# Four weight sums of a fast convolution moved from VectorE to ScalarE and an accumulating DMA, with the set-up in another order

## The chip, the cores and the metric

The kernel runs on one core of a Trainium2 chip. The metric is device time in microseconds: the median of three runs before is 747.08 us (746.89 to 747.51). A core has five engines with a queue each: TensorE (PE in the profile; its weight loads are PEld), VectorE (DVE), ScalarE (ACT), GpSimd (POOL) and SyncE (SP). An engine takes its instructions in order; semaphores tie the queues together.

## The reference

A causal convolution in time with eight matrix taps: each output row is a sum of eight input rows, each times a 512x512 matrix.

```python
B, S, D, K = 8, 4096, 512, 8          # x: (B, S, D), kernel: (K, D, D)
for k in range(K):
    shifted = x if k == 0 else np.concatenate([np.zeros((B, k, D)), x[:, :-k, :]], axis=1)
    out += np.matmul(shifted, kernel[k])
```

## The kernel before

**Layout.** The 32,768 rows are cut into 128 runs of 256 rows (16 runs per batch). A run is one partition's work: a matmul handles one time position of all 128 runs at once. `XR` is a ring of 20 time positions in transposed form (input features on partitions); a slice of it, or of a sum of such slices, is the stationary operand, and a weight tile of 128x512 in bf16 is the moving one. A product of a 512-wide input and a weight is four matmuls (`product`, L115). The result lands in a half of a PSUM pair (`pair`, two halves of 128x512 f32); there are four pairs.

**Arithmetic.** The first 4 positions of a run are computed directly with all eight taps (`direct`, 32 products). The other 252 are 21 steps of 12 positions. A step combines two groups of four taps, H1 and H0, with three groups of four positions by four nodes: PL uses the sum of the weight groups, MI their difference, H1 and H0 themselves. Inside a node four taps meet four positions, again by sums: weights have indices (b, c), each LO, HI or MID, where a MID weight is a difference of two others. For PL, MI and H1 a node is nine products: u (weight MID, MID), a0 and a1 (MID, LO and MID, HI), v0 and v1 (LO, MID and HI, MID), and l00, l01, l10, l11. H0 is a leaf: u, a0, a1 and eight more, so W[H0, LO, MID] and W[H0, HI, MID] aren't needed. The inputs of these products are sums of rows that VectorE makes: z, then A and s from z, and F from s.

**Course of a node.** a1 opens a PSUM pair q; ScalarE copies its half 1 to half 0 (L171, for the leaf L168 with a sign); u is added to half 1 and a0 to half 0. ScalarE then copies half 1 into two further pairs p0 and p1 (the seeds: L187, and L189 with a sign) and half 0 into the SBUF tile DT (`node_dts`, L193). TensorE adds v0 and v1, VectorE makes the other halves from DT (`node_d`), TensorE adds the l products, and `node_e` takes the pairs out: for PL by ScalarE (L229), for the others by VectorE. Node k is `nodes[k]`, counted from 1: node 1 is PL, 2 MI, 3 H1, 4 H0 of the first step, 5 PL of the second.

**Weights.** Eight taps are loaded by GpSimd's DMA queue with a cast to bf16 (`load_w`). All other weight tiles are made on the chip, once: 9 tiles for PL and MI each and the MID tiles of H1 and H0, by VectorE (`wsum` is a difference, `plus` a sum, both of 128x2048 bf16).

**Set-up.** Input rows come in two ways. Rows 0 to 11 of each run and the last seven rows of the run before (the history, for the first positions) are loaded by GpSimd or SyncE into tiles that later hold weights (`xin`, `H`, `XF`), transposed by TensorE into PSUM (`transpose_pe`, names x0, x4, x8, x9, h4, h3) and copied into `XR` by ScalarE (`here`, L296; `history`, L292, and a memset by VectorE). Later rows go to DRAM as bf16 (`load_x`) and into `XR` by SyncE's transposing DMA (`transpose_x`). `fill` issues two matmuls on a zero tile whose result isn't used. The first steps aren't a loop: the order of all instructions, for each queue, is the order of the calls from `pd = ...` (L378) to `go(4, "d1")` (L595), written out. `go(k, name)` is one act of node k's slot, and in it acts of the nodes after it; go(2, "s0"), say, is seed 0 of node 3, and go(2, "u") its u. From node 5 on a loop over `SLOT` (L597) gives the order. A load on GpSimd's queue waits for the landing of the one eight before it.

Of the kernel before, what the change touches and what calls it, by code (L numbers as in the profile page):

```python
# [14 lines left out]
def kernel(  # L15
# [64 lines left out]
    def tt(o, a, b, op):  # L80
        nc.vector.tensor_tensor(out=o, in0=a, in1=b, op=op)  # L81
# [7 lines left out]
    def rows(o, t, n):  # L89
        load(o, xr[:, t:t + n, :])  # L90
# [56 lines left out]
    def node_A(n):  # L147
        tt(AX[n.k % 2], n.z[:, n.o + 2:n.o + 4], n.z[:, n.o + 3:n.o + 5], ADD)
# [24 lines left out]
    def node_a0(n):  # L173
        product(n.q[:, 0], comps(n)[1][0], W[n.a, MID, LO], False)
# [76 lines left out]
    def load_w(tap):  # L251
        n = K - 1 - tap
        load(W[n >> 2, n >> 1 & 1, n & 1], kr[:, :, tap, :])

    def wsum(a, b_, c_):
        o = W[a, b_, c_]
        if a == MI and b_ != MID and c_ != MID:
            tt(o, W[H0, b_, c_], W[H1, b_, c_], SUB)
        elif b_ == c_ == MID:
            tt(o, W[a, MID, LO], W[a, MID, HI], SUB)  # L260
        elif b_ == MID:
            tt(o, W[a, HI, c_], W[a, LO, c_], SUB)
        else:
            tt(o, W[a, b_, LO], W[a, b_, HI], SUB)
# [7 lines left out]
    def fill(pw):  # L272
        for h in range(2):
            nc.tensor.matmul(pw[:, h], lhsT=zero[:, 0:P], rhs=zero, start=True, stop=True)  # L274

    def transpose_pe(name, k, src, t0, t1):
        o = pair(k).bitcast(bf).rearrange("p a (b d) -> p (a b) d", b=2)
        for t in range(t0, t1):
            for c in range(DC):
                nc.tensor.transpose(o[:, t - t0, c * P:(c + 1) * P], src[:, t, c * P:(c + 1) * P],  # L280
                                    ident)
        bank[name] = o[:, 0:t1 - t0]
# [7 lines left out]
    def history(eng, t, name):  # L290
        z = XR[:, place(t):place(t) + bank[name].shape[1]]
        eng(out=to(z), in_=prev(bank[name]))  # L292
        nc.vector.memset(z[:, :, 0:D:G], 0.0)

    def here(eng, t, name, a, b):
        eng(out=XR[:, place(t) + a:place(t) + b], in_=bank[name][:, a:b])  # L296
# [18 lines left out]
    def seed_plus(b_, c_):
        nc.scalar.copy(out=W[PL, b_, c_], in_=W[H1, b_, c_])

    def seed_minus(b_, c_):
        nc.scalar.mul(out=W[MI, b_, c_], in_=W[H1, b_, c_], mul=-1.0)

    def add_h0(a, b_, c_):
        nc.gpsimd.dma_start(out=W[a, b_, c_], in_=W[H0, b_, c_], accum_op=ADD)
# [50 lines left out]
    def go(k, name):  # L373
        there, act = step(k)[name]
        if there:
            act()

    pd = {0: pair(0), 1: pair(1)}  # L378
    load_w(0)
    rows(H[:, 4:8], RUN - 4, 4)  # L380
    make_identity(nc, ident)
    nc.vector.memset(zero, 0.0)
    nc.sync.dma_start(out=XF, in_=xr[:, 0:4, :])
    cast(nc.vector.tensor_copy, 2, 4)
    for k in range(7):
        fill(pair(2 + k % 2))
    go(3, "v1")
    cast(nc.scalar.copy, 0, 2)
    transpose_pe("x0", 2, xin[0], 0, 4)
    load_w(4)  # L390
    here(nc.scalar.copy, 0, "x0", 2, 4)
    go(3, "d0")
    load_w(5)
    load_w(1)
    here(nc.scalar.copy, 0, "x0", 0, 2)
    fill(pair(3))
    load_w(7)
    fill(pair(3))
    direct(0, 3)
    direct(0, 2)  # L400
    fill(pair(2))
    transpose_pe("h4", 3, H, 4, 8)
    history(nc.scalar.copy, -4, "h4")
    load_w(3)
    plus((HI, HI))
    wsum(H1, HI, MID)
    wsum(MI, HI, HI)
    plus((HI, LO))
    wsum(MI, HI, LO)
    direct(0, 1)  # L410
    direct(0, 0)
    direct(4, 3)
    fill(pair(2))
    wsum(PL, HI, MID)
    direct(4, 0)
    direct(4, 2)
    direct(4, 1)
    wsum(H1, MID, LO)
    wsum(MI, HI, MID)
    plus((LO, LO))  # L420
    direct(5, 3)
    wsum(MI, LO, LO)
    wsum(PL, MID, LO)
    load_w(6)
    direct(1, 0)
    rows(H[:, 1:4], RUN - 7, 3)
    direct(1, 3)
    direct(5, 1)
    direct(5, 2)
    direct(1, 1)  # L430
    direct(7, 3)
    direct(1, 2)
    direct(3, 3)
    direct(3, 2)
    direct(3, 0)
    wsum(H0, MID, LO)
    load_w(2)
    load_xin(4)
    wsum(H1, LO, MID)
    wsum(H1, MID, HI)  # L440
    wsum(H1, MID, MID)
    direct(6, 2)
    direct(3, 1)
    transpose_pe("h3", 2, H, 1, 4)
    history(nc.scalar.copy, -7, "h3")
    direct(6, 3)
    load_xin(8, 0, 2)
    direct(2, 2)
    direct(7, 2)
    plus((LO, HI))  # L450
    direct(2, 0)
    transpose_pe("x4", 3, xin[4], 0, 4)
    direct(2, 1)
    direct(7, 0)
    load_xin(8, 2, 4)
    wsum(PL, MID, HI)
    transpose_pe("x8", 2, xin[8], 0, 2)
    here(nc.scalar.copy, 4, "x4", 0, 2)
    here(nc.scalar.copy, 4, "x4", 2, 4)
    fill(pair(3))  # L460
    transpose_pe("x9", 2, xin[8], 2, 4)
    direct(7, 1)
    direct(6, 1)
    wsum(MI, LO, HI)
    direct(5, 0)
    wsum(PL, LO, MID)
    direct(6, 0)
    load_x(12)
    here(nc.scalar.copy, 8, "x8", 0, 2)
    wsum(MI, MID, HI)  # L470
    wsum(PL, MID, MID)
    wsum(MI, LO, MID)
# [8 lines left out]
    node_a1(nodes[1])
    load_x(20)
    load_x(24)
    s_rows(nodes[1], 0, 3)
    direct(2, 3)
    node_u(nodes[1])
    node_seed(nodes[1], 0)
    node_seed(nodes[1], 1)
    node_a0(nodes[1])
    node_dts(nodes[1])  # L490
    s_rows(nodes[1], 3, 5)
    transpose_x(12)
    node_z(nodes[2])
    node_A(nodes[2])
# [6 lines left out]
    wsum(MI, MID, LO)
    wsum(MI, MID, MID)
    node_a1(nodes[2])
    direct_out(1)
    go(1, "l00")
    go(1, "s")
    go(1, "l01")
    go(1, "e0")
    go(1, "a0")
    go(1, "dt")  # L510
    go(1, "u")
    go(1, "s0")
    go(1, "z")
    go(1, "F0")
    go(1, "A")
# [10 lines left out]
    go(1, "e1")
    wsum(H0, MID, HI)
    go(1, "a1")
    go(1, "d1")
    go(2, "s")  # L530
    go(2, "l00")
    go(2, "l01")
    go(2, "a0")
    go(3, "v0")
    go(2, "dt")
    go(2, "e0")
    go(2, "z")
    go(2, "u")
    go(2, "s0")
    go(2, "l10")  # L540
    go(2, "s1")
    go(1, "x")
    go(2, "x")
    wsum(H0, MID, MID)
# [16 lines left out]
    go(3, "l10")
    go(3, "s")
    go(3, "z")
    go(3, "A")
    go(3, "l11")
    go(3, "e1")
    go(4, "l01")
    go(3, "s1")
    go(3, "d1")
    go(4, "l00")  # L570
    go(4, "s")
    go(3, "dt")
    go(4, "b1")
    go(4, "l10")
    go(3, "g0")
# [4 lines left out]
    go(4, "s0")  # L580
    go(4, "a0")
    go(4, "s1")
    go(4, "F0")
    go(4, "dt")
    go(4, "z")
    go(4, "A")
    go(4, "v0")
    go(4, "l11")
# [41 lines left out]
```

## Time and profile before

| | |
|---|---|
| median of three runs | 747.08 us |
| profiled execution, its own time | 746.51 us |
| its span, from the first to the last instruction | 744.8 us |
| TensorE busy | 729.3 us, 98% |
| VectorE busy | 697.2 us, 94% |
| ScalarE busy | 241.3 us, 32% |
| GpSimd busy | 57.8 us, 8% |
| share of the chain that ended last: PE | 93% |

Busy time counts the time in which an engine works at an instruction. Matmuls overlap one another, and their ends are modelled, so a hole of TensorE is read best from one start to the next. The chain that ended last is followed back from the last instruction, at each step to what released it or to the instruction before it on its engine. A row of a timeline gives the start, the length, the engine, the line, the operation, the tiles (written <- read) and the count, and in brackets the idle time before it and what ended it.

### The profile page before, as it was taken

How to read it: one execution, taken by the hardware profiler on the slowest of the kernel's cores; microseconds unless marked ns; L12 is line 12 of the kernel's file. 1: busy time of each engine (PE TensorE's matmuls, PEld its weight loads, DVE VectorE, ACT ScalarE, POOL GpSimd, SP SyncE). 2: the span in 40 equal slices, each digit the busy share in tenths (PEclk: the TensorE clock that was granted, in tenths of full speed). 3: DMA queues.
4: the chain of work that ended last, by engine and by line, in shares of the span. 5: the costliest groups of instructions: out<-in, count | busy, mean ns of one | idle time of the engine just before them, and what ended most of it. 6: DMA issues, size and time to landing. Idle time of an engine off the chain costs nothing.

```text
span 744.8 us, 8881 instructions
## 1 busy us (share of the span) xinstructions
PE 729.3 (98%) x3354; PEld 331.0 (44%) x3422; DVE 697.2 (94%) x729; ACT 241.3 (32%) x369; POOL 57.8 (8%) x98
## 2 busy tenths in 40 slices
PE   8989999999999999999999999999999999999997
PEld 3444444444444444444444444444444444444443
DVE  2999999999999999999999999999999999999996
ACT  3053233332333333232423333242333323333331
POOL 5200010101010010101011010101101010100000
PEclk9999999999999999999999999999999999999999
DMA  9996859696877969697795969688596968865414
GB/s 199 210 214 161 225 118 251 136 234 162 203 205 163 236 145 235 156 219 182 185 231 138 233 152 236 165 181 239 137 240 142 241 164 188 220 148 179 139 78 170
DMA packets 159372, 138.88 MB, mean 186 GB/s; under 512 B 130144, under 2 KB 134240, under 8 KB 159200
## 3 DMA queue, kind: packets, MB, share of 16 engines
q1 hardware_dynamic: 145456, 99.89, 49.6%
q0 software_dynamic: 13728, 38.15, 28.0%
q8 instruction: 27, 0.44, 0.2%
q10 hardware_dynamic: 144, 0.26, 0.1%
q14 instruction: 17, 0.14, 0.1%
HBM read 77.33 MB, written 99.09 MB: 237 GB/s over the span
## 4 chain that ended last, share of the span: by engine, by line
PE 93%; ACT 1%; issue 1%; DVE 1%; DVEq 0%; ACTq 0%
PE pp L117 92%; ACT pp L187 0%; DVE w L81 0%; PE pp L280 0%; ACT DT L193 0%; ACT XR L296 0%; DVE pp L81 0%; DVE pp L206 0%; DVE y L81 0%; ACT pp L189 0%; DVEq L625 0%; ACT pp L168 0%; ACT pp L171 0%; PE pp L274 0%; DVE F L81 0%
## 5 line engine op out<-in xcount | busy, mean ns | idle before, releaser
L117 PE MATMUL pp<-w,S 128*128 128x512 bf16 x1153 | 269.0, 379 | 1.5
L117 PE MATMUL pp<-w,F 128*128 128x512 bf16 x986 | 248.4, 379 | 1.0
L117 PEld LDWEIGHTS <-S 128*128 128x128 bf16 x1176 | 114.8, 98 | 140.2 <-issue 3.6
L117 PE MATMUL pp<-w,A 128*128 128x512 bf16 x659 | 170.5, 379 | 2.7 <-ACT pp L189 1.2
L81 DVE TENSOR_TENSOR Z<-XR 128x2048 bf16<-128x2048 bf16 (+3 forms) x109 | 154.6, 1437 | 0.1
L117 PEld LDWEIGHTS <-F 128*128 128x128 bf16 x1008 | 98.6, 98 | 119.0
L81 DVE TENSOR_TENSOR S<-Z 128x2560 bf16<-128x2560 bf16 (+1 forms) x85 | 124.8, 1469 | 0.0
L187 ACT COPY pp<-pp 128x512 f32<-128x512 f32 x84 | 57.3, 682 | 158.8 <-PE pp L117 154.0
L117 PEld LDWEIGHTS <-A 128*128 128x128 bf16 x672 | 65.2, 97 | 82.8 <-DVE A L81 4.5
L171 ACT COPY pp<-pp 128x512 f32<-128x512 f32 x63 | 35.9, 570 | 198.9 <-PE pp L117 198.9
L117 PE MATMUL pp<-w,Z 128*128 128x512 bf16 x330 | 85.4, 379 | 1.7 <-ACT DT L193 1.4
L81 DVE TENSOR_TENSOR F<-S 128x1024 bf16<-128x1024 bf16 x126 | 86.6, 687 | 0.0
L106 POOL COPY junk<-A 128x2 bf16<-128x2 bf16 x18 | 17.6, 980 | 557.4 <-DVE A L81 557.4
L232 DVE SCALAR_TENSOR_TENSOR y<-pp,y 128x1024 f32<-128x1024 f32 x42 | 51.3, 1222 | 8.9 <-PE pp L117 8.4
L81 DVE TENSOR_TENSOR A<-Z 128x1024 bf16<-128x1024 bf16 x84 | 57.9, 690 | 1.5
L189 ACT ACTIVATE pp<-pp 128x512 f32<-128x512 f32 x84 | 58.1, 692 | 1.1 <-PE pp L117 1.1
L206 DVE SCALAR_TENSOR_TENSOR pp<-pp,DT 128x512 f32<-128x512 f32 x63 | 43.9, 697 | 14.5 <-PE pp L117 14.5
L229 ACT ACTIVATE y<-pp 128x1024 f32<-128x1024 f32 x42 | 43.1, 1027 | 40.3 <-PE pp L117 40.1
L81 DVE TENSOR_TENSOR y<-y,pp 128x1024 f32<-128x1024 f32 (+1 forms) x43 | 51.1, 1190 | 2.0 <-PE pp L117 1.9
L81 DVE TENSOR_TENSOR y<-pp,y 128x1024 f32<-128x1024 f32 x42 | 51.2, 1219 | 1.7 <-DMA out_dram<-y 1.7
L117 PEld LDWEIGHTS <-Z 128*128 128x128 bf16 x336 | 32.9, 98 | 41.4 <-issue 1.5
L247 DVE SCALAR_TENSOR_TENSOR y<-y 128x1024 f32<-128x1024 f32 x42 | 51.2, 1219 | 0.0
(28 smaller groups left out, 244.9 us busy)
## 6 DMA issues: line engine op xcount, KB each, us to landing
out_dram<-y SPq DMA_DIRECT2D x127, 512.0 KB, 7.7
xd<-in_x_dram POOLq DMA_DIRECT2D x61, 512.0 KB, 10.8
w<-in_kernel_dram POOLq DMA_DIRECT2D x8, 512.0 KB, 15.9
w<-in_x_dram SPq DMA_DIRECT2D x1, 1024.0 KB, 4.9
w<-in_x_dram POOLq DMA_DIRECT2D x2, 512.0 KB, 14.9
XR<-xd SPq DMA_TRANSPOSE x61, 5.4
w<-in_x_dram POOLq DMA_DIRECT2D x2, 256.0 KB, 18.4
w<-in_x_dram POOLq DMA_DIRECT2D x1, 384.0 KB, 20.3
```

Source lines behind the costliest of these rows:

```text
L81: nc.vector.tensor_tensor(out=o, in0=a, in1=b, op=op)
L106: nc.gpsimd.tensor_copy(out=junk, in_=z[:, 0:2])
L117: nc.tensor.matmul(bank, lhsT=comp[:, c * P:(c + 1) * P], rhs=w[:, c, :], start=start and c == 0, stop=c == DC - 1, skip_group_check=True)
L171: nc.scalar.copy(out=n.q[:, 0], in_=n.q[:, 1])
L187: nc.scalar.copy(out=o, in_=q)
L189: nc.scalar.mul(out=o, in_=q, mul=-1.0)
L206: nc.vector.scalar_tensor_tensor(out=p[:, 0], in0=p[:, 1], scalar=-1.0, in1=DT, op0=MUL, op1=SUB)
L229: nc.scalar.mul(out=cc[b_], in_=p, mul=0.5)
L232: nc.vector.scalar_tensor_tensor(out=dd[b_], in0=p, scalar=-0.5, in1=cc[b_], op0=MUL, op1=ADD)
L247: nc.vector.scalar_tensor_tensor(out=cc[b_], in0=cc[b_], scalar=2.0, in1=dd[b_], op0=MUL, op1=SUB)
```

## The change

Four weight tiles, W[H0, MID, HI], W[H0, MID, LO], W[H0, MID, MID] and W[H1, LO, MID], which VectorE made as a difference p - m, are now made in two steps: ScalarE writes -m into the tile (`wminus`), and a DMA on GpSimd's queue adds p to it (`wplus`, `accum_op=ADD`). Which two tiles are p and m stands in `terms`. Three helpers that were not called are gone. The calls of the set-up stand in another order: the taps are loaded 0, 1, 4, 5, 2, 6, 3, 7 instead of 0, 4, 5, 1, 7, 3, 6, 2, rows 4 to 11 before the last four taps, the history rows first; the direct products follow the taps; the row sums of nodes 1 and 2 stand among the weight sums; and the first acts of nodes 1 to 4 are permuted. The fills are 13 in both.

```diff
+    def terms(a, b_, c_):
+        if a == MI and b_ != MID and c_ != MID:
+            return W[H0, b_, c_], W[H1, b_, c_]
+        if b_ == c_ == MID:
+            return W[a, MID, LO], W[a, MID, HI]
+        if b_ == MID:
+            return W[a, HI, c_], W[a, LO, c_]
+        return W[a, b_, LO], W[a, b_, HI]
+
     def wsum(a, b_, c_):
-        o = W[a, b_, c_]
...
+        p, m = terms(a, b_, c_)
+        tt(W[a, b_, c_], p, m, SUB)
+
+    def wminus(a, b_, c_):
+        nc.scalar.mul(out=W[a, b_, c_], in_=terms(a, b_, c_)[1], mul=-1.0)
+
+    def wplus(a, b_, c_):
+        nc.gpsimd.dma_start(out=W[a, b_, c_], in_=terms(a, b_, c_)[0], accum_op=ADD)
```

The new order of the set-up, up to node 3, with what was there before left out:

```python
    nc.vector.memset(zero, 0.0)
    make_identity(nc, ident)
    nc.sync.dma_start(out=XF, in_=xr[:, 0:4, :])
    for k in range(7):
        fill(pair(2 + k % 2))
    fill(pair(3))
    ...
    rows(H[:, 4:8], RUN - 4, 4)
    ...
    load_xin(4)
    transpose_pe("x4", 3, xin[4], 0, 4)
    here(nc.scalar.copy, 4, "x4", 0, 2)
    load_xin(8, 0, 2)
    transpose_pe("x8", 2, xin[8], 0, 2)
    direct(1, 3)
    load_xin(8, 2, 4)
    transpose_pe("x9", 2, xin[8], 2, 4)
    here(nc.scalar.copy, 4, "x4", 2, 4)
    ...
    here(nc.scalar.copy, 8, "x8", 0, 2)
    wsum(PL, HI, MID)
    z_rows(nodes[1], 0, 5)
    ...
    wminus(H0, MID, HI)
    load_w(6)
    ...
    node_z(nodes[2])
    direct(3, 1)
    wminus(H1, LO, MID)
    wsum(MI, LO, HI)
    direct(6, 0)
    node_A(nodes[2])
    wminus(H0, MID, LO)
    plus((LO, LO))
    wsum(PL, MID, LO)
    wplus(H0, MID, LO)
    node_a1(nodes[1])
    ...
    node_seed(nodes[1], 0)
    node_v(nodes[1], 0)
    wsum(MI, MID, HI)
    node_a1(nodes[2])
    node_v(nodes[1], 1)
    ...
    go(1, "a1")
    go(1, "d0")
    go(1, "F0")
    go(1, "v1")
    load_x(20)
    go(1, "e1")
    wminus(H0, MID, MID)
    go(2, "u")
    go(1, "d1")
    wplus(H0, MID, MID)
    go(2, "s0")
    go(2, "a0")
```

Before, the corresponding calls around node 3 stood so: `go(2, "a0")`, `go(3, "v0")`, `go(2, "dt")`, `go(2, "e0")`, `go(2, "z")`, `go(2, "u")`, `go(2, "s0")`; and `wsum(MI, MID, HI)` stood ahead of node 1's z.

More of the change, by code (lines that the diff above doesn't have):

```diff
@@ L253, in load_w @@
         load(W[n >> 2, n >> 1 & 1, n & 1], kr[:, :, tap, :])
-    def wsum(a, b_, c_):
-        o = W[a, b_, c_]
[L257 to L264, printed above, removed]
+    def terms(a, b_, c_):
[6 more added lines that the diff above has]
+        return W[a, b_, LO], W[a, b_, HI]
+    def wsum(a, b_, c_):
+        p, m = terms(a, b_, c_)
[4 more added lines that the diff above has]
+        nc.gpsimd.dma_start(out=W[a, b_, c_], in_=terms(a, b_, c_)[0], accum_op=ADD)
     def plus(*which):
@@ L313, in direct_out @@
         store(2 * b_, y)
[L315 to L322, printed above, removed]
     def z_rows(n, a, b):
@@ L378 @@
     pd = {0: pair(0), 1: pair(1)}
-    load_w(0)
-    rows(H[:, 4:8], RUN - 4, 4)
+    nc.vector.memset(zero, 0.0)
     make_identity(nc, ident)
-    nc.vector.memset(zero, 0.0)
     nc.sync.dma_start(out=XF, in_=xr[:, 0:4, :])
-    cast(nc.vector.tensor_copy, 2, 4)
+    go(3, "v0")
     for k in range(7):
         fill(pair(2 + k % 2))
-    go(3, "v1")
+    fill(pair(3))
+    cast(nc.vector.tensor_copy, 2, 4)
+    rows(H[:, 4:8], RUN - 4, 4)
     cast(nc.scalar.copy, 0, 2)
     transpose_pe("x0", 2, xin[0], 0, 4)
-    load_w(4)
@@ L391 @@
-    here(nc.scalar.copy, 0, "x0", 2, 4)
-    go(3, "d0")
-    load_w(5)
-    load_w(1)
-    here(nc.scalar.copy, 0, "x0", 0, 2)
-    fill(pair(3))
[L397 to L407, printed above, removed]
-    plus((HI, LO))
[L409 to L413, printed above, removed]
@@ L414 @@
-    wsum(PL, HI, MID)
[L415 to L472, printed above, removed]
+    here(nc.scalar.copy, 0, "x0", 0, 2)
+    load_w(0)
+    here(nc.scalar.copy, 0, "x0", 2, 4)
+    fill(pair(3))
+    transpose_pe("h4", 3, H, 4, 8)
+    fill(pair(2))
+    direct(0, 1)
+    rows(H[:, 1:4], RUN - 7, 3)
@@ new lines @@
+    fill(pair(2))
+    transpose_pe("h3", 2, H, 1, 4)
+    history(nc.scalar.copy, -4, "h4")
+    direct(0, 2)
+    history(nc.scalar.copy, -7, "h3")
+    load_w(1)
+    direct(0, 3)
+    direct(0, 0)
+    direct(1, 0)
+    go(3, "v1")
+    load_w(4)
+    load_w(5)
+    wsum(MI, HI, HI)
+    plus((HI, HI))
+    direct(1, 1)
+    direct(1, 2)
+    direct(4, 2)
+    wsum(H1, HI, MID)
+    direct(4, 0)
+    direct(4, 3)
+    wsum(MI, HI, LO)
+    direct(4, 1)
+    direct(5, 2)
+    direct(5, 0)
+    load_xin(4)
@@ L473 @@
+    transpose_pe("x4", 3, xin[4], 0, 4)
+    go(4, "x")
+    here(nc.scalar.copy, 4, "x4", 0, 2)
+    load_xin(8, 0, 2)
+    go(3, "d0")
+    transpose_pe("x8", 2, xin[8], 0, 2)
+    direct(1, 3)
+    load_xin(8, 2, 4)
+    transpose_pe("x9", 2, xin[8], 2, 4)
+    here(nc.scalar.copy, 4, "x4", 2, 4)
+    direct(5, 1)
+    fill(pair(3))
+    load_w(2)
+    plus((HI, LO))
+    wsum(MI, HI, MID)
+    direct(2, 2)
+    direct(2, 1)
+    here(nc.scalar.copy, 8, "x8", 0, 2)
+    wsum(PL, HI, MID)
     z_rows(nodes[1], 0, 5)
-    load_x(16)
@@ L475 @@
-    node_A(nodes[1])
+    direct(2, 3)
     here(nc.scalar.copy, 10, "x9", 0, 2)
     z_rows(nodes[1], 5, 7)
+    s_rows(nodes[1], 3, 5)
     fill(pair(2))
-    go(4, "F1")
-    direct_out(0)
[L481 to L486, printed above, removed]
-    node_seed(nodes[1], 0)
[L488 to L494, printed above, removed]
@@ L495 @@
-    node_F(nodes[1], 0)
+    wminus(H0, MID, HI)
+    load_w(6)
+    s_rows(nodes[1], 0, 3)
+    node_F(nodes[1], 0)
+    load_w(3)
+    node_A(nodes[1])
+    plus((LO, HI))
+    load_w(7)
+    direct(2, 0)
+    wplus(H0, MID, HI)
+    direct(6, 2)
+    wsum(PL, MID, HI)
+    direct(6, 3)
+    node_z(nodes[2])
+    direct(3, 1)
+    wminus(H1, LO, MID)
+    wsum(MI, LO, HI)
+    direct(6, 0)
+    node_A(nodes[2])
+    wminus(H0, MID, LO)
+    plus((LO, LO))
+    wsum(PL, MID, LO)
+    wplus(H0, MID, LO)
@@ L496 @@
+    node_a1(nodes[1])
+    direct(5, 3)
+    direct(7, 0)
+    wsum(PL, MID, MID)
+    direct(3, 0)
+    wplus(H1, LO, MID)
+    direct(3, 3)
+    direct(6, 1)
+    wsum(PL, LO, MID)
+    wsum(MI, LO, LO)
+    direct(7, 1)
+    wsum(H1, MID, HI)
+    node_u(nodes[1])
+    load_x(12)
+    go(3, "d1")
+    wsum(MI, MID, LO)
+    node_a0(nodes[1])
+    direct(3, 2)
+    direct_out(0)
+    node_seed(nodes[1], 1)
+    go(1, "s")
+    node_dts(nodes[1])
+    direct(7, 2)
+    node_seed(nodes[1], 0)
     node_v(nodes[1], 0)
+    wsum(MI, MID, HI)
@@ L497 @@
+    node_a1(nodes[2])
+    node_v(nodes[1], 1)
     node_d(nodes[1], 0)
+    wsum(MI, MID, MID)
     go(1, "F1")
-    node_v(nodes[1], 1)
-    node_d(nodes[1], 1)
[L501 to L508, printed above, removed]
+    go(1, "z")
+    direct(7, 3)
+    go(1, "A")
+    go(1, "l01")
+    go(1, "u")
+    go(1, "l00")
+    direct_out(1)
+    go(1, "s0")
+    node_d(nodes[1], 1)
     go(1, "a0")
@@ L510 @@
     go(1, "dt")
[L511 to L515, printed above, removed]
+    go(1, "e0")
     go(1, "l11")
+    transpose_x(12)
+    wsum(MI, LO, MID)
+    wsum(H1, MID, LO)
     go(1, "s1")
-    load_x(28)
+    wsum(H1, MID, MID)
+    load_x(16)
     go(1, "l10")
     go(1, "v0")
-    load_x(32)
+    go(1, "a1")
+    go(1, "d0")
+    go(1, "F0")
     go(1, "v1")
+    load_x(20)
+    go(1, "e1")
+    wminus(H0, MID, MID)
+    go(2, "u")
+    go(1, "d1")
+    wplus(H0, MID, MID)
@@ L523 @@
+    go(2, "s0")
+    go(2, "a0")
+    go(2, "s")
     go(3, "F0")
-    go(1, "d0")
+    go(2, "l00")
     go(2, "F1")
[L526 to L531, printed above, removed]
-    go(2, "l01")
[L533 to L544, printed above, removed]
+    go(2, "z")
+    go(2, "dt")
+    go(2, "l01")
@@ L547 @@
     go(2, "d0")
-    go(2, "v1")
-    go(2, "d1")
-    go(2, "a1")
+    go(2, "l10")
+    go(2, "e0")
+    go(1, "x")
+    go(3, "s")
     go(2, "l11")
+    go(2, "s1")
     go(2, "A")
     go(3, "l00")
+    go(3, "l01")
+    go(2, "a1")
+    go(2, "v1")
+    go(2, "e1")
     go(3, "F1")
-    go(3, "l01")
+    go(3, "a0")
+    go(2, "d1")
+    go(3, "e0")
     go(3, "u")
-    go(2, "e1")
-    go(3, "e0")
-    go(3, "a0")
-    go(3, "s0")
[L561 to L565, printed above, removed]
+    go(3, "s1")
+    go(3, "z")
+    go(4, "s")
+    go(3, "A")
+    go(3, "l10")
+    go(3, "dt")
+    go(3, "l11")
+    go(4, "z")
+    load_x(24)
+    load_x(28)
+    go(4, "F0")
+    go(2, "x")
+    go(3, "g0")
+    load_x(32)
+    go(3, "s0")
     go(3, "e1")
+    go(4, "l11")
+    go(4, "l10")
+    go(4, "l00")
+    go(4, "b1")
     go(4, "l01")
[L568 to L575, printed above, removed]
     go(4, "u")
-    go(4, "x")
+    go(4, "a0")
+    go(4, "s0")
     go(4, "e0")
-    load_x(36)
[L580 to L588, printed above, removed]
+    go(4, "g1")
+    go(4, "s1")
+    go(4, "v0")
+    go(4, "A")
+    go(4, "v1")
+    go(4, "dt")
+    go(4, "d0")
+    go(4, "F1")
+    load_x(36)
+    go(4, "d1")
     go(3, "r")
-    go(4, "g1")
-    go(4, "v1")
-    go(4, "d0")
+    go(4, "a1")
     go(4, "e1")
-    go(4, "a1")
-    go(4, "d1")
     for k in range(5, len(nodes)):
```

## The prediction

> **What bounds the kernel now.** I read TensorE's busy time by stage first, then its waits, then the engines' timelines over the first 90 us. By stage (range, length, busy with count, clock, DMA share, GB/s):
>
> ```profile
> 0.00:20.00 20.00, 17.64 (x89) 1.00 1.03 199
> 20.00:40.00 20.00, 18.44 (x110) 1.00 1.15 211
> 40.00:60.00 20.00, 17.89 (x86) 1.00 1.01 216
> 60.00:80.00 20.00, 19.22 (x88) 1.00 0.54 121
> 80.00:100.00 20.00, 19.18 (x88) 1.00 0.93 246
> ```
>
> TensorE is the bound from start to end: the chain that ended last is 93% PE, and from 200 to 700 us it is busy 99.5 of every 100 us. All loops after the set-up are untouched and the number of matmuls is equal (26 fills and 76 transposes among them), so the change is worth what it does to TensorE's holes before about 90 us. Four of the holes in TensorE's timeline:
>
> ```profile
> 40.07 0.61 PE L280 MATMUL pp<-ident,w 128*128 128x128 bf16 x8 [0.67 <-ACT XR L296]
> ...
> 48.38 1.02 PE L117 MATMUL pp<-w,A 128*128 128x512 bf16 x4 [1.21 <-ACT pp L189]
> ...
> 63.91 1.02 PE L117 MATMUL pp<-w,Z 128*128 128x512 bf16 x4 [0.68 <-ACT DT L193]
> ...
> 82.05 1.02 PE L117 MATMUL pp<-w,A 128*128 128x512 bf16 x4 [0.70 <-ACT pp L187]
> ```
>
> A row is a group, its start, length, and in brackets the idle time and what ended it. The idle time counts from a modelled end; start to start, less 0.216 per matmul, each hole is 0.16 longer. So counted, before loses 0.63 in four small holes up to 12.8 us, then 0.83 (15.31), 0.33 (32.29), 0.85 (34.00), 0.83 (40.07), 1.38 (48.38), 0.89 (55.31), 0.84 (63.91), 0.87 (82.05): 7.45 us.
>
> None of these waits for a weight sum. Most wait for ScalarE, and three show a rule needed below. At 63.91 the product u writes half 1 of node 3's PSUM pair, but waits for DT's copy, which reads half 0; at 48.38 and 82.05 a0 writes half 0 and waits for seeds that read half 1. A product waits for every reader of its pair queued before it, whichever half. ScalarE and VectorE:
>
> ```profile
> 36.83 1.93 ACT L296 COPY XR<-pp 128x1024 bf16<-128x1024 bf16 x2 [4.10 <-PE pp L280]
> 39.01 1.01 ACT L296 COPY XR<-pp 128x1024 bf16<-128x1024 bf16 x1 [0.25 <-PE pp L280]
> ...
> 60.74 0.57 ACT L171 COPY pp<-pp 128x512 f32<-128x512 f32 x1 [1.62 <-PE pp L117]
> 63.27 0.59 ACT L193 COPY DT<-pp 128x512 f32<-128x512 f32 x1 [1.97 <-PE pp L117]
> ```
>
> ```profile
> 37.36 1.22 DVE L81 TENSOR_TENSOR w<-w 128x2048 bf16<-128x2048 bf16 x1
> 38.50 1.22 DVE L81 TENSOR_TENSOR w<-w,w 128x2048 bf16<-128x2048 bf16 x1
> 39.63 1.22 DVE L81 TENSOR_TENSOR w<-w 128x2048 bf16<-128x2048 bf16 x1
> ```
>
> ScalarE has room (1.6 to 2 us idle between two of its steps); VectorE has hardly any from 19 to 95 us, a sum each 1.135 us.
>
> **The skill.** "TensorE: Matmul & The Clock Gate", Part 1 (warmup), gives a matmul of 512 columns 426.7 ns start to start cold and 215.7 warm: the first 14 fills here take 5.98 us (0.427 each), later ones 0.216. "ScalarE: Activation LUTs", What ACT_TABLE_LOAD costs, gives 186 + 0.833 N ns with an immediate scale: 1.04 us at N = 1024, against 1.01 to 1.03 here. "DMA: Bandwidth & Descriptors", SDMA does more than copy, says that an inline unit adds two streams; it gives no rate, and no accumulating DMA is in this trace.
>
> **The change, part by part.** Prices: a product of 4 matmuls 0.863; a sum 1.135; ScalarE's copy of 128x512 0.57, of 128x1024 0.92 back to back. A negated copy of 128x2048 is not in the trace: 0.44 more per 512 columns gives 1.89, the page's formula 1.89 as well; back to back 1.80.
>
> *Removed:* four sums, 4 x 1.135 = 4.5 us of VectorE. Worth nothing by itself, as no hole waits for them; it counts only if VectorE ends a hole in the new order.
>
> *Loads.* The bytes up to the last tap are the same. GpSimd's queue starts a further load 0.25 us after each landing, so these are read off:
>
> ```profile
> 9.40 0.55 POOL L87 DMA_DIRECT2D w<-in_x_dram  x1 [1.26 <-DMA w<-in_kernel_dram]
> 11.86 0.74 POOL L87 DMA_DIRECT2D w<-in_kernel_dram  x1 [1.91 <-DMA w<-in_x_dram]
> 14.45 0.54 POOL L87 DMA_DIRECT2D w<-in_x_dram  x1 [1.84 <-DMA w<-in_kernel_dram]
> ```
>
> So 512 KB take about 2.5 us. In the new order: history rows 9.1, tap 0 11.6, the other history rows 13.45, tap 1 16, tap 4 18.5, tap 5 21 to 22, rows 4 to 7 24.5, rows 8 and 9 25.7, 10 and 11 27, tap 2 29.5, tap 6 32, tap 3 34.5, tap 7 37.2. The identity is made first (0.6 us of GpSimd): I take 0 for it, since the first queued packets are held behind the 1 MB of SyncE's load (landed 5.64; the first packet of GpSimd's queue moves at 4.87); at most 0.6.
>
> *Start, up to 28.65.* Fourteen cold fills as before (7.18), two warm ones and x0's transposes (0.89) end at 8.6. The fill after h4's transposes waits for both x0 copies, 10.83: 0.78 lost with 0.2 small ones. Tap 0 costs 0.33, the second history rows 0.55. From 13.5: h3's 12 transposes 0.67 and 12 products, 24.5: rows 4 to 7 have just landed. Their two copies (1.93), then x8's (1.0), hold x9's transposes, which share x8's bank, until 28.65: 0.35 + 1.6 lost, where before loses 0.83 at 40.07.
>
> *Middle.* From 28.65 TensorE has x9's transposes 0.45, two fills 0.86 and 21 products 18.1, with 0.25 for node 1's seed: 48.3. Next is node 2's a1, which needs W[MI,MID,HI]. VectorE starts node 1's z only when x8 is copied (28.65); then come z, s, F and A of nodes 1 and 2 (1.40 + 0.60 + 1.93, 0.60 + 0.83 + 1.40, 0.60, 2 x 0.60, each from its row: 8.6), 11 sums (12.5), 0.5 until x9 is copied and 0.5 between dependent ones: 50.75. TensorE stands 2.15 more. Before had this sum at 39.6; it is now late although four sums are gone, since VectorE idles about a microsecond before 28.65 and row sums now precede it.
>
> *Node 3.* Thirteen products on, at 61.95, a0 of node 3 is due. The new order queues seed 0 between u and a0, so by the rule a0 waits for it; ahead of it on ScalarE stand node 1's output copy and the negated copy for W[H0,MID,MID]. Node 3's a1 starts 50.75 + 10 x 0.863 = 59.4; its copy ends 1.11 + 0.57 later, 61.0; output copy 61.9; negated copy 63.7; seed 64.3. Lost: 2.35, where before loses 0.84 at u. VectorE's F of node 3 and all of TensorE are queued behind.
>
> *Other negated copies* (30 to 36.8) run while ScalarE has nothing due until node 1's a1 (39): nothing.
>
> *Accumulations.* Bounded by 1.2 us each (half a load's traffic) and 5 (twice); I take 2.5, as one reads two bf16 rows per row written, the bytes of an f32 row load. The first three land by 45; the first user is node 3's v0 at 67: hidden, with 20 us of cover. The fourth is issued at 63.75 and needed by node 4's first product at 71.15, a cover of 7.4: row loads land 4.4 us after issue at the least and 7.4 in the median, so it is just hidden; past that each microsecond is lost on TensorE, with all that is queued there. The x loads behind these on GpSimd's queue land at 47 to 53 and, for rows 24 on, 71; SyncE's transpose of row 12 stands behind the second output store anyway (55), and the stores behind row 24's transpose are due at 81.
>
> *Sum.* After: 0.98 + 0.33 + 0.55 + 0.35 + 1.6 + 0.25 + 2.15 + 2.35, and 0.87 at node 5's seed as before, is 9.4; 9.4 - 7.45 = +2.0. The other way: a0 at 64.3 and 14 products bring node 4's outer products to 76.4, against 74.28 for the same count of matmuls before: +2.1. I take +2.05. The profiled run took 746.51 with a span of 744.8, so 748.6 and 746.9; on the median of 747.08, 0.57 above that run, 749.1.
>
> **Rivals.** *VectorE is not late (same).* If W[MI,MID,HI] is ready by 48.3, 2.4 us sooner than I sum, 2.15 falls away and the rest is -0.1: 747.0. For it: four sums less, and 8.6 us of row sums priced from single rows. Against: copies of x rows set VectorE's restart. It decides from 0.6 us of that (0.2%, 1.5 us, being about what a measurement here can tell from no change). *The accumulation is slow (slower still).* At 5 us instead of 2.5 the median landing is 73.65, 2.5 lost: 751.6. *Neither late sum nor late seed (faster).* Both large holes gone, 4.5 us: 744.6; it needs ScalarE's seed by 61.95, against the order of its queue. That the sums do not move at all is excluded by the order as built.
>
> **How the numbers follow.** My case 0.55, its own range 748.1 to 750.1; slow accumulation 0.13; VectorE on time 0.23; both gone 0.09. An eighth of my case lies within 0.2%, so slower 0.62, same 0.27, faster 0.11. The range 746.6 to 751.4 leaves out the last case and the worst accumulations.
>
> **What would show it.** Right: idle before node 2's a1 (about 50.7) ended by a VectorE weight sum, about 2; idle before node 3's a0 (64) ended by ScalarE's seed, about 2.2, with a 1.9 us activation just ahead of it; x9's transposes at 28.65. Wrong: those products start without idle, or a wait on the accumulated tile at node 4's first product (71).

## The result and the profile after

The changed kernel takes 749.74 us in the median of eight executions (749.12 to 750.79); the kernel before 747.15 in eight (746.41 to 747.90). The ratio is 1.0034, 95% interval 1.0025 to 1.0044; in the medians the change is slower by 2.6 us, where 2.05 was forecast. Ratios here and below are taken over the executions and not from the medians; one execution each of "a0 before its seed" and "all edits at once", over 1.5% above the fastest of its kernel, is left out of them. The profiled execution took 750.74 us with a span of 749.0, 4.2 more than before's 744.8. It is one of the three of eight with a mean TensorE clock of 0.997, all at 750.0 or above; the five at 0.999 or 1.0 lie at 749.1 to 749.8. That difference is a finding of its own, below.

TensorE by stage, in the kernel after (range, length, busy with count, clock, DMA share, GB/s):

```profile
0.00:20.00 20.00, 15.58 (x95) 1.00 1.02 201
20.00:40.00 20.00, 18.27 (x108) 1.00 1.15 205
40.00:60.00 20.00, 17.47 (x72) 0.91 0.81 173
60.00:80.00 20.00, 17.69 (x81) 1.00 1.00 192
80.00:100.00 20.00, 19.29 (x89) 1.00 1.06 281
```

The first four stages lost busy time: the first 2.06 us (in part because its fills were over sooner, see the balance below), the fourth 1.53. The third has a clock of 0.91, where before had 1.00 everywhere. TensorE's timeline of the kernel after, the rows with an idle time of over 0.4 us:

```profile
9.29 1.07 PE L288 MATMUL pp<-ident,w 128*128 128x128 bf16 x16 [1.19 <-DMA w<-in_x_dram]
11.92 1.02 PE L117 MATMUL pp<-w,XR 128*128 128x512 bf16 x4 [1.35 <-DMA w<-in_kernel_dram]
13.87 0.84 PE L288 MATMUL pp<-ident,w 128*128 128x128 bf16 x12 [0.49 <-DMA w<-in_x_dram]
28.89 0.61 PE L288 MATMUL pp<-ident,w 128*128 128x128 bf16 x8 [1.62 <-ACT XR L304]
51.11 1.02 PE L117 MATMUL pp<-w,A 128*128 128x512 bf16 x4 [2.43 <-DVE w L81]
66.40 1.02 PE L117 MATMUL pp<-w,A 128*128 128x512 bf16 x4 [2.20 <-ACT pp L187]
88.88 1.89 PE L117 MATMUL pp<-w,S 128*128 128x512 bf16 x8 [0.66 <-ACT pp L187]
```

The forecast named the two large ones: at 51.11 node 2's a1 waits for a weight sum of VectorE, at 66.40 node 3's a0 for a seed of ScalarE. What stands ahead of each, on VectorE and then on ScalarE of the kernel after:

```profile
48.44 1.48 DVE L81 TENSOR_TENSOR S<-Z 128x2560 bf16<-128x2560 bf16 x1
49.84 1.22 DVE L81 TENSOR_TENSOR w<-w,w 128x2048 bf16<-128x2048 bf16 x1
```

```profile
63.04 1.03 ACT L229 ACTIVATE y<-pp 128x1024 f32<-128x1024 f32 x1
63.95 1.91 ACT L269 ACTIVATE w<-w 128x2048 bf16<-128x2048 bf16 x1
65.75 0.60 ACT L187 COPY pp<-pp 128x512 f32<-128x512 f32 x1
```

The sum that ends at 51.06 releases a1 at 51.11; the negated copy (1.91 us) stands right ahead of the seed, and a0 follows the seed. GpSimd's queue, which the experiments turned out to be about:

```profile
36.62 1.76 POOL L272 DMA_DIRECT2D w<-w  x2 [3.03 <-ACT w L269]
37.75 2.24 POOL L87 DMA_DIRECT2D xd<-in_x_dram  x3
66.17 0.91 POOL L272 DMA_DIRECT2D w<-w  x1 [26.17 <-ACT w L269]
66.74 2.42 POOL L87 DMA_DIRECT2D xd<-in_x_dram  x4
```

For 26.17 us GpSimd waits for the negated copy, and behind it wait four loads of x rows (24 to 36). In the kernel before, all seven of these loads (rows 12 to 36) had been issued by 36.8.

**The balance.** Start to start, less 0.216 per matmul, after has 0.36, 1.36, 1.29, 0.65, 1.78, 0.06, 0.16, 2.59, 2.37 and 0.82 us of holes: 11.4, against 7.45 before, so +4.0. (The trace has 25 of the 26 fill matmuls; the one that is missing, at 10.20, is counted.) Full clock came sooner at the start: at 4.43 us, with eight matmuls a step of 0.43 or nearly so apart, against 6.86 and fourteen in the kernel before: −1.3. That isn't a gain of the change, since full clock begins anywhere from 3.8 to 6.9 us in the fourteen profiled executions of all kernels. And the clock is halved from 52.2 to 55.6: about +1.7. Together +4.4, against +4.2 in the spans.

### The profile page after: what moved, and what is told of

Same layout as the page of the kernel before. It is cut to its first block, busy times and chain, and to the rows that moved or that the text cites. A ratio compares the mean times of both kernels' runs of the same rounds, so it can differ in the third digit from the quotient of the medians.

```text
span 749.0 us, 8893 instructions
## 1 busy us (share of the span) xinstructions
PE 729.4 (97%) x3354; PEld 331.3 (44%) x3422; DVE 692.7 (92%) x725; ACT 248.4 (33%) x373; POOL 62.2 (8%) x102
## 4 chain that ended last, share of the span: by engine, by line
PE 90%; DVE 2%; issue 1%; ACT 1%; DVEq 0%; ACTq 0%
PE pp L117 90%; DVE w L81 1%; DVE Z L81 0%; DVE y L81 0%; ACT pp L187 0%; ACT pp L168 0%; DVE y L247 0%; ACT y L229 0%; DVE S L81 0%; DVE pp L81 0%; DVEq L628 0%; DVE F L81 0%; ACT pp L171 0%; ACT w L269 0%; DVEq L81 0%
```

## The experiments

Theory: TensorE's queue stands twice, once for VectorE's late sum and once for ScalarE's seed behind a negated copy, and that is the loss. Rivals: the substitution itself (ScalarE's or the DMA's work) costs the time; VectorE is late as a whole, so that mending one wait opens the next; the half clock has another cause. The runs were made in four groups, each beside the kernel before on its chip, whose median lay between 746.5 and 747.4; so ratios are compared.

| run | median us | ratio to before, 95% interval | executions at clock 0.998 or less |
|---|---|---|---|
| the changed kernel | 749.74 | 1.0034 (1.0025 to 1.0044) | 3 of 8 |
| order alone | 752.21 | 1.0073 (1.0060 to 1.0086) | 4 of 5 |
| substitution alone | 748.05 | 1.0020 (1.0012 to 1.0027) | 2 of 14 |
| W[H1,MID,HI] later | 749.13 | 1.0029 (1.0018 to 1.0040) | 4 of 7 |
| two products first | 748.59 | 1.0034 (1.0022 to 1.0047) | 2 of 5 |
| a0 before its seed | 748.97 | 1.0054 (1.0028 to 1.0079) | 15 of 15 |
| copy early | 754.59 | 1.0108 (1.0093 to 1.0124) | 4 of 4 |
| loads early | 753.74 | 1.0090 (1.0075 to 1.0104) | 4 of 4 |
| copy early, loads held | 748.29 | 1.0017 (1.0010 to 1.0023) | 12 of 21 |
| hole filled | 749.48 | 1.0043 (1.0030 to 1.0055) | 2 of 5 |
| copy early, loads held, hole filled | 747.23 | 1.0001 (0.9993 to 1.0009) | 3 of 13 |
| all edits at once | 758.91 | 1.0123 (1.0088 to 1.0157) | 6 of 6 |
| all edits, loads later | 753.12 | 1.0087 (1.0073 to 1.0101) | 5 of 5 |

### The two halves of the change apart

*The order alone:*

```diff
-    wminus(H0, MID, HI)        (and the other three wminus)
-    wplus(H0, MID, HI)         (and the other three wplus, each at its place)
+    wsum(H0, MID, HI)
```

> The new order alone: the four sums are VectorE's again, each where its accumulating DMA is issued; no negated copies. My theory: three of them (3.4 us) come ahead of W[MI,MID,HI], whose hole grows from 2.6 to 6.0 us; node 3's a0 no longer waits behind a negated copy, 1.5 less: +1.9 against the changed kernel, 751.0 with full clock and up to 752.7 with the half clock after the hole. Rival, the substitution itself costs the time and the order is harmless: 747.6 or less.

Measured: 752.21, in the range expected. TensorE's timeline:

```profile
45.84 1.04 PE L117 MATMUL pp<-w,Z 128*128 128x512 bf16 x4 [1.82 <-DVE w L81]
54.05 1.02 PE L117 MATMUL pp<-w,A 128*128 128x512 bf16 x4 [3.56 <-DVE w L81]
67.85 1.02 PE L117 MATMUL pp<-w,A 128*128 128x512 bf16 x4 [0.71 <-ACT pp L187]
```

VectorE's lateness grew by the three sums as expected, only that it is paid in two places: 1.99 at node 1's u and 3.72 at node 2's a1 (start to start), 5.7 where 6.0 were expected; and the hole at node 3's a0 is down to 0.88. The new order without the substitution costs 0.73%, with it 0.34%: in this order the substitution is worth about 2.9 us. So it isn't what makes the change slow here.

*The substitution alone*, for three of the four sums, in the order before:

```diff
-    wsum(H0, MID, LO)
+    wminus(H0, MID, LO)
...
-    wsum(H1, LO, MID)
+    wminus(H1, LO, MID)
...
     history(nc.scalar.copy, -7, "h3")
+    wminus(H0, MID, HI)
...
     load_x(32)
+    wplus(H0, MID, LO)
+    wplus(H1, LO, MID)
+    wplus(H0, MID, HI)
...
-    wsum(H0, MID, HI)
```

> The substitution alone, in the order of the kernel before: W[H0,MID,LO], W[H1,LO,MID] and W[H0,MID,HI] by ScalarE's negated copy (two in its idle stretch before 31 us, one between 33 and 37) and an accumulating DMA behind the last x load (36 us), without the fourth; 3.4 us less on VectorE. My theory, no hole of the kernel before waits for VectorE's weight sums, and no negated copy stands before a seed here: 746.5, within 0.5 of the kernel before. Rival one, relief of VectorE is worth time: 1 to 2 us less. Rival two, the accumulations disturb the transposes that follow: 748 or more.

Measured: 748.05, ratio 1.0020. Neither the theory (no effect) nor the first rival (1 to 2 us less): the second rival. Three sums less on VectorE did not gain time as a whole; the run costs 1.3 us. In its VectorE timeline:

```profile
65.82 1.23 DVE L81 TENSOR_TENSOR Z<-XR 128x2048 bf16<-128x2048 bf16 x1 [2.05 <-DMA XR<-xd]
66.96 1.22 DVE L81 TENSOR_TENSOR w<-w,w 128x2048 bf16<-128x2048 bf16 x1
```

SyncE's first transpose keeps its queue for 15.74 us, where before had 9.89 (with the accumulations ahead of it, the last x load is issued at 42.24 instead of 36.25); the row sum z waits for the transposed row, the sum W[H0,MID,MID] stands behind it, and TensorE's u of node 4 at 68.23 waits 0.58 for that (0.73 from start to start). So the profile places somewhat over half of the 1.3 us there, by way of the accumulations; the rest isn't placed.

### How late VectorE is

```diff
-    wsum(H1, MID, HI)
     node_u(nodes[1])
...
     wsum(MI, LO, MID)
+    wsum(H1, MID, HI)
     wsum(H1, MID, LO)
```

> VectorE's sum W[H1,MID,HI] (1.13 us) moves from ahead of W[MI,MID,HI] to the three sums at 56.6 us, behind which VectorE stands for 1.5 us anyway. My theory, VectorE's work ahead of the late sum is what counts: the hole of 2.59 us at node 2's a1 falls to 1.45, and all that VectorE makes up to 58 us comes 1.13 sooner: 748.6 in the median, 748.0 with full clock. Rival, VectorE is held by other things there (TensorE's own products, S): less than 0.4 is gained; or the sum is late for node 3's a1 at 61.4, a new hole.

Measured: the hole at node 2's a1 is 1.63 (2.59 in the changed kernel), no new hole at node 3, and the three executions at full clock take 747.35 to 748.44, 1.1 above the kernel before in the middle where the changed kernel's are 2.0 to 2.7 above. In the median, with four of seven at a lower clock, 749.13, so the gain is only seen at equal clock. The hole shrank by 0.96, about one sum: what VectorE does ahead of W[MI,MID,HI] sets the hole.

```diff
-    node_a1(nodes[2])
     node_v(nodes[1], 1)
+    direct(7, 3)
+    node_a1(nodes[2])
```

(and `direct(7, 3)` taken away further down)

> Two products that need no late weight (v of node 1's second half, and tap 7 of head row 3) go ahead of node 2's a1 in TensorE's queue, 1.73 us of work; the sum W[MI,MID,HI] stays as late as it is. My theory, TensorE only stands because a1 is next in its queue: the hole of 2.59 us falls to about 0.9, and without so long a hole the clock is not halved after it: 747.4 in the median, all runs within 0.8 us. Rival, VectorE is late as a whole, so that the time is only lost at its next product for TensorE (u of node 2, F): 749 or more.

Measured: 748.59, and against its own kernel before no gain at all (1.0034). The hole did shrink, and another opened; TensorE's timeline:

```profile
50.57 1.02 PE L117 MATMUL pp<-w,A 128*128 128x512 bf16 x4 [0.70 <-DVE w L81]
56.18 1.89 PE L117 MATMUL pp<-w,F 128*128 128x512 bf16 x8 [1.10 <-DVE pp L206]
```

Of the 1.73 us that TensorE won at a1 it lost 1.26 again at 56.18, where a product of node 1 waits for VectorE's `node_d`. The rival is right for the most part: by the profile VectorE as a whole is late in this stretch, and a reordering of TensorE's queue alone only moves the wait.

### The seed behind the negated copy

```diff
-    go(2, "s0")
     go(2, "a0")
+    go(2, "s0")
```

> Node 3's a0 is queued ahead of its seed 0, so that by my rule it waits only for the copies of its pair queued before it (done at 63.1 us); the negated copy and its DMA stay where they are. My theory: the hole of 2.37 us at a0 falls below 0.3, 2.1 less: 747.6 in the median, 747.0 with full clock. Rival, a0 needs the seed's data or VectorE is as late as ScalarE there: the hole moves to the next product of node 3 or to F, and less than 0.8 is gained (749 or more).

Measured: the hole at a0 is gone, so a0 doesn't need the seed's data, and what held it was the seed queued before it on the same PSUM pair. But TensorE then stands later:

```profile
71.20 1.04 PE L117 MATMUL pp<-w,Z 128*128 128x512 bf16 x4 [0.79 <-DMA w<-w]
```

This is node 4's u, waiting for the fourth accumulating DMA (issued 65.5, landed 5.7 us later). In the changed kernel it landed at 71.83 and was needed at 73.31: 1.5 us to spare, which is less than the 2.4 that a0 came earlier. Ten of fifteen executions take 747.0 to 750.0 (nine of them at 0.998), five take 756.1 to 758.2. The profile is of the first kind; what the five met was not seen.

```diff
     node_seed(nodes[1], 0)
+    wminus(H0, MID, MID)
...
     go(1, "e1")
-    wminus(H0, MID, MID)
```

> Only the negated copy for W[H0,MID,MID] moves, from just ahead of node 3's seed 0 to ScalarE's empty stretch after node 1's seeds (it is idle from 47.6 to 52.2 us); the accumulating DMA stays where it is. My theory, ScalarE's queue holds the seed and the seed holds a0: the hole at node 3's a0 falls from 2.37 us to about 0.85 (as in the kernel before at u), so 1.5 us less than the changed kernel: 748.2 in the median, 747.6 where the clock is full. Rival, a0 is held by something else there (a late row sum of VectorE, or the transfer): no change, 749.7.

Measured: 754.59, 5 us slower than the changed kernel instead of 1.5 faster. The hole at a0 did fall, to 0.88. The loss is elsewhere; GpSimd's, SyncE's and VectorE's timelines, one after the other:

```profile
49.00 0.91 POOL L272 DMA_DIRECT2D w<-w  x1 [9.21 <-ACT w L269]
49.57 2.43 POOL L87 DMA_DIRECT2D xd<-in_x_dram  x4
```

```profile
56.15 17.28 SPq L94 DMA_TRANSPOSE XR<-xd  x3
```

```profile
71.72 1.22 DVE L81 TENSOR_TENSOR Z<-XR 128x2048 bf16<-128x2048 bf16 x1 [6.52 <-DMA XR<-xd]
```

The copy was not all that moved. The accumulating DMA waits for it on GpSimd's queue, and the loads of rows 24 to 36 wait behind that; they now enter at 49.57 instead of 66.74. The three transposes issued from 56.15 on keep their queue for 17.28 us (7.45 in the changed kernel), the row sum z waits 6.52 for them, and TensorE, at 74.20, 4.88 for VectorE. (In this profile the clock also fell to half twice, at the hole before node 2's a1 and at this one.) That was a new theory, with the early accumulation itself as its rival. Two runs tell them apart.

```diff
     wplus(H0, MID, MID)
+    behind(cc[1][:, 0])        # GpSimd copies two elements of node 1's last output
```

(with the early copy as above)

> As in the run with the copy made early, which took 754.6 us, but GpSimd then makes a two-element copy that waits for node 1's last output copy (ScalarE, 64 us), so that the loads of rows 20 to 32 are issued at about 64.5 us, near their 66.7 in the changed kernel, while the accumulating DMA goes at 49. New theory, the early copy let those loads in at 49.6 us, in front of the transposes that node 3's and 4's row sums need: the wait of 6.5 us is gone, and with the hole at a0 down to 0.85 the time is 748.2 in the median. Rival, the early accumulation (512 KB, issued at 49.0) is what delays the transposes: 753 or more.

Measured: 748.29, and 746.96 in the median of the nine executions at clock 1.0. The loads enter at 63.37, the hole at a0 is 0.88, and VectorE doesn't wait for a transposed row. The accumulation still goes at 49, so it isn't the cause. The other way round, the loads early and the copy where it was:

```diff
     load_x(20)
+    behind(W[MI, MID, HI][:, 0])
+    load_x(24)
+    load_x(28)
+    load_x(32)
+    load_x(36)
     go(1, "e1")
```

(and these four loads taken away further down)

> The changed kernel with its negated copies and accumulating DMAs untouched; only the loads of rows 24 to 36 are queued on GpSimd ahead of the fourth accumulation and behind a two-element copy that waits for W[MI,MID,HI] (51 us), so that they enter at about 51.5 us instead of 66.7. Theory: those loads alone delay the transposes of rows 12 to 20, and VectorE's row sum Z of node 4 waits for them: 752 to 755, with a wait of VectorE for a transposed row of 3 to 7 us. Rival, in the run with the early copy it was the accumulation: no change, 749.5.

Measured: 753.74 (751.42 to 755.23); the loads entered at 51.19, the three transposes took 16.96 us, and z waited 2.93 for them in the profiled execution, the fastest of the four. So early loads are enough by themselves. In the changed kernel the wait for the negated copy, which costs TensorE 1.5 us at a0, also kept the loads out of the transposes' way.

### The half clock

In the profiled execution of the changed kernel TensorE's clock fell to half right after the hole at 51.11. Windows of 4 us (range, length, busy, clock, DMA share, GB/s):

```profile
48.00:52.00 4.00, 1.57 (x9) 1.00 1.03 266
52.00:56.00 4.00, 3.95 (x11) 0.57 0.30 59
56.00:60.00 4.00, 4.00 (x20) 1.00 0.61 170
```

From 52.22 to 55.63 matmuls start 0.427 us apart: 3.41 us at half clock, 1.7 us lost, which is the step between the two groups of executions. Does it follow the hole?

```diff
+    def hold(pw, n):           # 2 n matmuls whose result is overwritten
+        for k in range(n):
+            for h in range(2):
+                nc.tensor.matmul(pw[:, h], lhsT=ident, rhs=W[1, 1, 1][:, 0], start=True, stop=True)
...
+    hold(pair(3), 5)
     node_a1(nodes[2])
```

> Ten matmuls whose result is overwritten (2.16 us) are queued ahead of node 2's a1, so that TensorE works through the hole of 2.59 us instead of standing; nothing comes sooner. My theory, the half clock from 52.22 to 55.63 us follows the idle hole: it is gone, the clock is 0.999 or more in every run, and the runs lie at 749.1 to 749.8 with none at 750 or above: 749.2 in the median. Rival, the half clock has another cause: the same scatter, 749.7 in the median, clock 0.997 in a third of the runs.

Measured: a miss. The hole is filled (0.27 us idle), yet two of five executions have a clock of 0.997 and take 750.6 and 750.9. But the hole of 2.37 at a0 was still there, and could do the same. So both were taken away, by this edit and those of the run with the early copy and the loads held together:

> The run with the early copy and the loads held, with the ten overwritten matmuls (2.16 us) ahead of node 2's a1 as well: the longest stretch without a matmul after 20 us is then the one of about 1.5 us at 28.4. In the run with the early copy and the loads held alone, 11 of 21 executions had a clock of 0.998 or less, at 748.5 in their median, and 10 a clock of 1.0, at 746.96. Theory, a stretch of over 2 us without a matmul is what the half clock follows in some executions: hardly any execution at 0.998 or less, and 747.0 in the median. Rival, the half clock has another cause: about half of the executions at 0.998 or less, 748.3 in the median.

Measured: 747.23, ratio 1.0001, against 1.0017 for the same kernel without the ten matmuls, with intervals that don't overlap. None of thirteen executions is below 0.998, three are at it (747.7 to 748.2). Without the ten matmuls it was 12 of 21, with nine at full clock; the expectation has 11 and 10. Nothing in this edit makes anything ready sooner, so ten useless matmuls are worth 1.2 us by the ratios, for the most part through the clock. (At full clock the two kernels lie 0.2 above and 0.3 below their kernels before, on two chips; that half a microsecond isn't explained.) The expected count (hardly any at 0.998) was not quite met, and the kernel before, whose longest hole after 20 us is 1.4, had such a clock in 8 of its 84 executions. So a stretch without matmuls is shown as a cause, not as the only one.

The Trainium skill, "TensorE: Matmul & The Clock Gate", Part 1, says that the clock halves after at least one idle window of about 3.4 us, in windows that run freely. The 3.41 us of the half clock agree with the window's length. The hole was 2.6 us, less than a window, and was followed by the half clock only in some executions. The measurement decides: here a hole shorter than the window is enough at times.

The traces also say at which times. In all fourteen profiled executions the clock changes only at whole multiples of 3.413 us after it first became full; in the changed kernel that was at 4.43 us, and 14 such stretches later, at 52.22, it halved. First the two stretches of the changed kernel around that moment, then those around the same hole in the profile of the run with the early copy and the loads held:

```profile
48.81:52.22 3.41, 1.11 (x6) 1.00 1.05 285
52.22:55.63 3.41, 3.41 (x9) 0.50 0.26 50
```

```profile
46.16:49.58 3.42, 2.07 (x9) 1.00 1.05 231
49.58:52.99 3.41, 2.33 (x11) 1.00 1.07 261
```

Both holes are 2.59 us long. In the changed kernel 2.31 of it lay in one stretch, and the half clock followed; in the other it was cut into 1.51 and 1.08, and the clock stayed full. After 20 us this holds in all fourteen: from full clock, the half clock followed where 2.08 us or more of a hole lay in one stretch, and not where it was 1.84 or less. So which executions lose the clock depends on where the hole falls among these stretches. This is read from the traces; no run sets it, and what shifts the stretches from one execution to the next was not seen.

### All edits at once

The early copy with the loads held, W[H1,MID,HI] later, two products first, a0 before its seed, and

```diff
     load_xin(8, 2, 4)
+    here(nc.scalar.copy, 8, "x8", 0, 2)
     transpose_pe("x9", 2, xin[8], 2, 4)
```

(taken away further down)

> All that the runs point to at once: negated copy early with the loads held, W[H1,MID,HI] later, two products ahead of node 2's a1, x8's copy ahead of x4's second, a0 of node 3 ahead of its seed. From the holes of the changed kernel after 24 us (7.8 us): the one at 28.9 falls from 1.8 to 0.8, the one at node 2's a1 with what follows from 2.6 to about 1.0, the one at a0 from 2.4 to nothing, 0.8 at node 5 stays: 2.6, so 5.2 less than 749.1 with full clock: 744, and no half clock. Rival, VectorE bounds that stretch, so that what TensorE gains is lost at the next row sum: 746 or more.

Measured: 758.91, the worst of all (751.12 to 765.49). The profiled execution is the longest, 765.49, so the sizes below are at the upper end. Up to 74.2 us TensorE is no later than in the kernel before: node 4's outer products start at 74.19 (74.28 there). Then it stands 16 us at 95.61, behind a row sum of VectorE that waits 18.30 for a transposed row. The loads were issued at 61.48, while the three transposes were under way (53.29 on, 17.56 us of SyncE's queue). DMA queues from 60 to 72 us: first the changed kernel, then this run (q1 carries the transposes and stores, q0 the loads; packets, MB, share of 16 engines):

```profile
q1 hardware_dynamic: 5633, 1.42, 58.2%
q0 software_dynamic: 190, 0.71, 38.2%
```

```profile
q1 hardware_dynamic: 3273, 0.83, 87.1%
q0 software_dynamic: 89, 0.34, 33.7%
```

A packet of q1 took 0.582 x 16 x 12 us / 5633 = 20 ns in the changed kernel and 51 ns here, so that the engines were at least as busy and moved half as much (178 and 98 GB/s). In the records from 64 to 76 us the transposes' packets of 256 bytes take 188 to 320 ns in the mean of 4 us, against 18 to 20 in the changed kernel. Loads under way at the same time slow the transposes down here, and not just by their share.

The last run put only the loads later, behind VectorE's output sum of node 2:

```diff
-    behind(cc[1][:, 0])
...
     go(2, "e0")
+    behind(dd[0][:, 0])
```

> The run with all edits at once (758.9 in its median), with one thing changed: the loads of rows 24 to 36 wait for a later step, VectorE's second output sum of node 2 (about 66.4 us in that run), and so enter at about 67.5 instead of 61.5, when the three transposes issued from 53.3 on should be over. Theory, loads and transposes that run at the same time slow each other down, and that alone made the loss: the stall of 16 us at 95 us is gone, node 4's outer products start at 73.3 to 73.8 (74.3 in the kernel before), 746.2 in the median, some 0.5 to 1 us under the kernel before. Rival, the new order of products and sums is itself what fails: 751 or more.

Measured: 753.12. Half of the expectation holds: node 4's outer products start at 73.39, 0.9 before the kernel before, the transposes' packets stay at 20 ns from 60 to 68 us, and the 16-us stall is gone. So the order of products and sums wasn't what failed. But now row 24's transpose, issued at 75.13, met loads: the four issued from 68.8 on, and three more issued from 77.34 on. It landed 17.9 us after its issue. SyncE, ScalarE and TensorE, then the DMA queues from 80 to 90 us:

```profile
75.13 13.57 SPq L94 DMA_TRANSPOSE XR<-xd  x1
88.80 3.39 SPq L218 DMA_DIRECT2D out_dram<-y  x5
```

```profile
94.22 1.02 ACT L229 ACTIVATE y<-pp 128x1024 f32<-128x1024 f32 x1 [7.10 <-DMA out_dram<-y]
95.14 0.59 ACT L187 COPY pp<-pp 128x512 f32<-128x512 f32 x1
```

```profile
95.78 3.57 PE L117 MATMUL pp<-w,S 128*128 128x512 bf16 x8 [5.00 <-ACT pp L187]
```

```profile
q0 software_dynamic: 528, 1.95, 97.2%
q1 hardware_dynamic: 526, 0.13, 9.7%
```

The transpose holds SyncE's queue, five output stores wait behind it, ScalarE waits for an output tile to be stored, and the seed behind that is late for TensorE. While both queues have work, their packets come about one for one, here and from 54 to 62 us of the substitution alone (426 and 440): a load's packet of 4096 bytes for each of the transpose's 256. From 90 to 92 us, with hardly any load left, q1 moves 1250 packets. So here few of the transpose's packets got through, at about 30 ns each; in the run before they took longer as well, and why isn't shown. The loads have a window of a few microseconds: after the transposes of rows 12 to 20 and early enough to be over before that of row 24. Whether all edits with the loads in that window beat the kernel before was not tried; no version run does.

## Why the prediction was right

By its steps, against the profiled execution and the runs:

- *The start up to x9's transposes at 28.65:* measured 28.89. The sum was right, its terms were not. "Fourteen cold fills as before" failed: full clock came at 4.4 us (6.9 before), by chance of the execution, which gave back 1.3 us; the DMAs came no sooner, so TensorE waited for them instead, 1.36 and 1.29 where the forecast has 0.78 and 0.33. That the two errors nearly cancel is luck. The 1.6 at x9's transposes measured 1.78, and the 0.35 for rows 4 to 7 didn't occur.
- *Node 2's a1 at 50.75 after a hole of 2.15:* 51.11 and 2.59, released by VectorE's weight sum. The working (row sums ahead of it, a restart with x8's copy) stands: one sum less ahead of it took 0.96 off. Its last subtraction does not: 50.75 less 48.3 is 2.45, which is nearer to what came, and would have made the whole +2.3.
- *Node 3's a0, 2.35:* 2.37, by the seed behind a negated copy of 1.91 us (1.89 forecast). The rule, a product waits for every reader of its pair queued before it, is shown by a0 ahead of the seed, without a hole.
- *Accumulations, 2.5 us and the fourth just hidden:* it landed 5.7 us after its issue (7.4 in the forecast), with 1.5 to spare. That the cover was near its end is shown where a0 came 2.4 earlier, and u of node 4 then waited for this DMA. The rival of a slow accumulation fell.
- *Four sums less "worth nothing by itself":* right for the order before as a whole, where the substitution alone gained nothing; in the new order, where VectorE ends a hole, it is worth 2.9 us, the case that the step left room for.
- *The rivals* of a punctual VectorE and of neither hole fell with the two waits in the profile.

The reading that no hole of the kernel before waits for a weight sum missed one. VectorE, then TensorE of the kernel before:

```profile
28.78 6.21 DVE L81 TENSOR_TENSOR w<-w,w 128x2048 bf16<-128x2048 bf16 x5
33.81 0.14 DVE L293 MEMSET XR<- 128x96 bf16 x1
```

```profile
34.00 1.90 PE L117 MATMUL pp<-w,XR 128*128 128x512 bf16 x7 [0.69 <-DVE XR L293]
```

The memset stands among five weight sums, though ScalarE's copy that it follows had ended at 32.73. With two sums fewer ahead of it (the substitution alone) the hole is 0.49 instead of 0.85. That is too little to change the forecast.

Two things were missing. The half clock after the holes isn't in the sum: 1.7 us in three of eight executions. It accounts for the 0.6 by which the median is above the forecast, as the five others have a median of 749.1; but the holes came to 2.0 more than forecast there, and the sooner full clock at the start took 1.3 of it back, so the close hit owes something to chance. And the loads behind the accumulating DMA were placed (71 us for rows 24 on) but judged by when they are needed alone; that their being held back protects the transposes came out only when the copy was moved.

## What to carry to other kernels

When a step is moved earlier, list what its queue-mates release with it: here a copy 16 us earlier let four loads into the transposes, which cost 5 us where 1.5 were to be won. A DMA queue that waits can be doing useful work as a gate; if the gate goes, put another in its place, and mind both ends of the window. On an engine that bounds the kernel, a hole of 2.6 us cost another 1.7 through the clock in part of the executions, so it can pay to keep the engine at useless work while it waits (1.2 us here).

## What the runs showed of the hardware

- Transposing DMAs from SyncE and loads from GpSimd share engines, as the Trainium skill's "DMA: Bandwidth & Descriptors", Issuing engines are not separate DMA queues, states ("interleave with each other"). The size was unexpected: with loads arriving in the middle of the transposes, packets of 256 bytes took 188 to 320 ns (means of 4 us) instead of 20, and the core's DMA moved 98 GB/s instead of 178 with its engines at least as busy. In another run the packets of the two queues came one for one (526 and 528 in 10 us), 256 bytes for 4096.
- An accumulating DMA of 512 KB within SBUF landed 5.7 us after its issue, 8.1 when x loads and stores were under way.
- A hole of 2.6 us was followed by 3.41 us of half clock in some executions and not in others, with the same instructions. In the fourteen traces it followed where at least 2.08 us of a hole after 20 us lay in one of the 3.413-us stretches counted from the first full clock, and not at 1.84 or less (read, not tested).
